# Fixed places behind named loads for the experts' side work, and another division of PSUM

## The chip, the cores and the metric

The kernel runs on one core of one Trainium2 chip. The metric is the device time of one execution in microseconds (us); lower is better. The engines are named as the profile names them: PE is TensorE's matmul, PEld its weight load, DVE is VectorE, ACT is ScalarE, POOL is GpSimd, and SP is SyncE, which here only issues transfers. An engine's issuing sequencer has a q behind its name (SPq).

## The reference, cut to what matters

One layer on 256 tokens of width 2048: a mixing sub-layer (three token mixers behind one projection, gated, summed, projected back), then a mixture of experts. Only the second half is touched by the change:

```python
combine = ...                      # (256 tokens, 16 experts), two weights per token are not zero
y = jnp.zeros_like(t)
for e in range(N_EXPERTS):         # 16 experts
    act = jax.nn.silu(t @ w_gate[e]) * (t @ w_up[e])      # 2048 -> 1024
    y = y + combine[:, e:e + 1] * (act @ w_down[e])       # 1024 -> 2048
x = x + gate_f * y
```

All is float32. An expert's three matrices are 8 MB each, so the 16 experts read 384 MB, which is most of what the kernel reads.

## The kernel before

**Stages.** Up to about 700 us the projections and mixers run; then the output projection, interleaved with the router's inputs; from about 850 us the router's choice; from about 865 us to the end the 16 experts. The kernel is written in a framework that sets the semaphores itself and fixes each engine's instruction order ahead of the run: it walks the program in order of priority with its own model of time, so an instruction whose inputs are ready in that model can be put ahead of one that was traced earlier. `tc.issue_after(ins)` adds an edge of order alone: what is traced in its block on the engine of `ins` comes behind `ins` on that engine.

**Experts.** A token's rows are not run through all experts: each expert has 64 slots (`CAP`). `gather` (matmuls L1071, one-hot `O` against the three bfloat16 parts `h2`) collects the tokens of an expert into `X`, transposed; L1077 and L1079 make their scale `rB`; DVE L1081 and L1083 scale and shift. `scatter` (L1096, ACT L1098) makes `OT`, the same one-hot the other way round.

A *unit* (L1118) multiplies 64 slots by a 128-row-pair slice of weights: one *load* `k2` is 1 MB (L855, issued by SP into the next of the rotating buffers `wr`, `m`, `ws`), and `pair` (L1111) issues its matmuls, 8 instructions in the trace, in two column halves of the array. The gate and the up matrix are a unit of 8 loads each, the down matrix two units (halves) of 4 loads. A unit's sums lie in one PSUM tile of two banks. Behind a unit:

- after gate or up, `hidden` copies the tile to `graw` (ACT L1133) and `rest` turns it round with matmuls (L1138, 16 instructions); then ACT applies Silu (L1146, tile `sgt`) or DVE multiplies (L1152, tile `A`);
- after a half of down, DVE L1164 scales it into `graw`, `split_to` cuts it into two parts `y` (ACT L173, DVE L174), and `combine_part` (two code matmuls L1176 and DVE L1177) adds a 128-token by 512-column part to the result `x2`. An expert has 8 such parts.

The units follow in the order gate(0), then for each expert e: up(e), gate(e+1), down(e) in two halves. The last expert's down matrix is read in another shape, 8 loads in 4 chunks of 512 columns; after each chunk `give_out` combines the chunk before it and sends it out through ACT's queue.

**Side work.** The pieces that stand between units (the gather, `scatter`, `rest`, the parts of combine) are closures in two lists, `soon` and `todo`. After each load's matmuls `between` (L1103) takes one piece off the lists. No edge ties a piece to the load after which it was traced.

**PSUM.** It has 8 banks. Before the experts two pools are closed and one is opened, so that the experts have three unit tiles (`ring`, 6 banks) and two single banks (`mx2`) for all the side work.

**Weight buffers.** 15 buffers of 1 MB rotate in the experts (18 until the first up unit is traced). SP's queue issues a load when the buffer's last reader on PE is done.

Of the kernel before, what the change touches and what calls it, by code (L numbers as in the profile page):

```python
# [53 lines left out]
def kernel(  # L54
# [988 lines left out]
    dve.tensor_copy(xr_i, xr_f)  # L1043

    fnp.close()
    mxbp.close()
    dn.close()


    ringp, ring_pool = open_pool(name="ring", bufs=3, space=PSUM)  # L1050

    def mx2():
        t = mx_pool.tile([P, 512], F32, name="mx")
        return t

    moep, moe = open_pool(name="moep", bufs=2, side="right")
    def ring():
        t = ring_pool.tile([P, 2, 512], F32, name="ring")
        return t

    def gather(O, Or, X, kg=8):

        for g in range(KD // kg):
            ps = mx2()
            for kk in range(kg):
                k2, j = divmod(g * kg + kk, 2)
                o = ps[:, kk * CAP:(kk + 1) * CAP]
                i = 0
                for t in range(NT):
                    for part in h2:  # L1070
                        pe.matmul(o, lhsT=part[:, t, k2 * 256 + j:(k2 + 1) * 256:2], rhs=O[:, t, 0:CAP],  # L1071
                                  start=i == 0, stop=i == 5)
                        i += 1
            if g == 0:
                pr = mx2()
                for t in range(NT):
                    pe.matmul(pr[:, 0:CAP], lhsT=ones, rhs=Or[:, t, :], start=t == 0, stop=t == NT - 1)  # L1077
                rB = moe.tile([P, 1, CAP], F32, name="rB", bufs=1)
                act.copy(rB[:, 0, :], pr[:, 0:CAP])  # L1079
            ks = slice(g * kg, (g + 1) * kg)  # L1080
            dve.tensor_tensor(X[:, ks, :], ps[:, 0:kg * CAP].rearrange("p (k s) -> p k s", s=CAP),  # L1081
                              rB.to_broadcast([P, kg, CAP]), op=ALU.mult)
            dve.tensor_tensor(  # L1083
                X[:, ks, :], X[:, ks, :],
                shT[:, ks].rearrange("p (k o) -> p k o", o=1).to_broadcast([P, kg, CAP]), op=ALU.add)
            yield
# [4 lines left out]

    def scatter(O):

        ps = mx2()
        for t in range(NT):
            pe.matmul(ps[:, t * P:(t + 1) * P], lhsT=O[:, t, :], rhs=ident_b, start=True, stop=True)  # L1096
        OT = moe.tile([P, S], F32R, name="OT", bufs=3)
        act.copy(OT, ps[:, 0:S])  # L1098
        return OT

    soon, todo = [], []

    def between():  # L1103
        for jobs in (soon, todo):
            if jobs:
                return jobs.pop(0)()

    def pair(acc, cc, lhs, k, rhs, last):

        for j in range(2):  # L1110
            pe.matmul(acc[j * CAP:(j + 1) * CAP, cc, :], lhsT=lhs[:, k + j, :], rhs=rhs[j],  # L1111
                      start=k == 0, stop=k == last)

    def drain():
        while soon:
            between()

    def unit(lhs, view, nk2):  # L1118


        acc = ring()
        for k2 in range(nk2):
            raw = load_e(view(k2))
            for cc in range(2):
                pair(acc, cc, lhs, 2 * k2, [raw[:, j * 1024 + cc * 512:j * 1024 + (cc + 1) * 512]
                                            for j in range(2)], 2 * nk2 - 2)
            between()
        return acc

    def hidden(acc):  # L1130

        raw = moe.tile([P, 1024], F32, name="graw", bufs=1)
        act.copy(raw, acc.rearrange("p a b -> p (a b)"))  # L1133

        def rest():
            ps = mx2()
            for b in range(8):
                pe.matmul(ps[:, b * CAP:(b + 1) * CAP], lhsT=raw[:, b * P:(b + 1) * P], rhs=id2[:, 0:CAP],  # L1138
                          start=True, stop=True)
            return ps.rearrange("p (k s) -> p k s", s=CAP)  # L1140
        return rest

    def gate_unit(wg, X):
        rest = hidden(unit(X, lambda k2: wg[:, k2], 8))
        sg = moe.tile([P, 8, CAP], F32, name="sgt", bufs=1)
        soon.insert(0, lambda: act.activation(sg, rest(), AF.Silu))  # L1146
        return sg

    def up_unit(wu, X, sg):
        rest = hidden(unit(X, lambda k2: wu[:, k2], 8))  # L1150
        A = moe.tile([P, 8, CAP], F32, name="A", bufs=1)
        soon.insert(0, lambda: dve.tensor_tensor(A, rest(), sg, op=ALU.mult))  # L1152
        return A

    def flush():
        while soon or todo:
            between()

    def down_unit(wd, A):
        ys = []  # L1160
        for hf in range(2):
            acc = unit(A, lambda k2: wd[:, k2, :, hf * 1024:(hf + 1) * 1024], 4)
            y = moe.tile([P, 1024], F32, name="graw", bufs=1)
            dve.tensor_tensor(y, acc.rearrange("p a b -> p (a b)"), late[0][:, hf * 1024:(hf + 1) * 1024],  # L1164
                              op=ALU.mult)
            yp = late[1].tile([P, 2, 1024], F32R, name="y", bufs=2)
            split_to(yp[:, 0, :], yp[:, 1, :], y)
            ys.append(yp)
        return ys

    def combine_part(OT, cme, parts, n, t):

        cl = slice(n * 512, (n + 1) * 512)
        ps = mx2()
        for i, y in enumerate(parts):
            pe.matmul(ps, lhsT=OT[:, t * P:(t + 1) * P], rhs=y, start=i == 0, stop=i == len(parts) - 1)  # L1176
        dve.scalar_tensor_tensor(x2[:, t, cl], ps, cme[:, t, :], x2[:, t, cl], op0=ALU.mult, op1=ALU.add)  # L1177

    def combine(OT, cme, ys):
        for n in range(4):  # L1180
            parts = [ys[n // 2][:, i, n % 2 * 512:(n % 2 + 1) * 512] for i in range(2)]
            for t in range(NT):
                todo.append(lambda n=n, t=t, parts=parts: combine_part(OT, cme, parts, n, t))

    state = {}

    def prepare(e, kg=8):

        rke = rank[:, :, e:e + 1]
        X = x_tile()  # L1190
        state[e] = [X, None]
        O, Or = (one_hot(rke), slot_scale(rke)) if e else (O0, Or0)
        parts = gather(O, Or, X, kg)

        def weights():
            state[e][1] = scatter(O)
        return [lambda: next(parts, 0)] * (KD // kg) + [weights]

    jobs = prepare(0, 4)
    jobs[0]()  # L1200
# [1 line left out]
    h2_rest(0, late_parts[0])  # L1202
    with tc.issue_after(slot_scale.last.ins), tc.issue_after(sigm.ins):
        h2_rest(1, late_parts[1])
    soon += jobs[2:]
    sg = gate_unit(wg_v[0], state[0][0])
    for e in range(NE - 1):
        soon += prepare(e + 1)
        A = up_unit(wu_v[e], state[e][0], sg)
        if e == 0:  # L1210
            rotate([pl for pl in rot[0] if pl is not wraw2])
            wr2p.close()
            latep, lt = open_pool(name="latep", bufs=1, side="left")
            late.append(lt.tile([P, D], F32, name="gfB"))
            late.append(lt)
            row_bcast(late[0], 3, 0, D)
        sg = gate_unit(wg_v[e + 1], state[e + 1][0])
        assert len(soon) == 1
        combine(state[e][1], cmb[:, :, e:e + 1], down_unit(wd_v[e], A))


    A, OT = up_unit(wu_v[NE - 1], state[NE - 1][0], sg), state[NE - 1][1]
    while todo:
        todo.pop(0)()
    flush()
    OT, cme = OT.bitcast(F32), cmb[:, :, NE - 1:NE]
    y_last = late[1].tile([P, D], F32, name="y", bufs=2)
    wl_v = w_e_down[0, NE - 1].rearrange("(b p) n -> p b n", p=P)

# [5 lines left out]

    for n in range(4):
        cl = slice(n * 512, (n + 1) * 512)
        acc = ring()
        for b0 in (0, 4):
            raw = load_e(wl_v[:, b0:b0 + 4, cl], 4)  # L1240
            for b in (0, 2):
                pair(acc, 0, A, b0 + b, [raw[:, (b + j) * 512:(b + j + 1) * 512] for j in range(2)], 6)
            if n and b0 == 0:
                give_out(n - 1)
        dve.tensor_tensor(y_last[:, cl], acc[:, 0, :], late[0][:, cl], op=ALU.mult)
    give_out(3)

# [1 line left out]
    with tc.If(nc.values_load(xr_i[0:1, NE:NE + 1], min_val=0, max_val=3) > 0):  # L1249
        with tc.For_i(0, NE) as ev:  # L1250
# [5 lines left out]
            with tc.For_i(0, nr):  # L1256
                dve.tensor_scalar(rke, rke, -float(CAP), None, op0=ALU.add)
                O, X = one_hot(rke), x_tile()
                OT = scatter(O)
                list(gather(O, slot_scale(rke), X))  # L1260
                sg = gate_unit(wg_v[bass.ds(ev, 1)][0], X)
                flush()
                A = up_unit(wu_v[bass.ds(ev, 1)][0], X, sg)
                flush()
                combine(OT, cme, down_unit(wd_v[bass.ds(ev, 1)][0], A))
                flush()
        sp.dma_start(out=out_v, in_=x2)


# [25 lines left out]
```

## Time and profile before

| | |
|---|---|
| median of 3 runs | 1851.79 us (1849.91 to 1852.36) |
| the profiled execution: its own time | 1852.96 us |
| its span, first to last instruction | 1851.2 us |
| PE, PEld busy | 1733.7 us (94%), 1050.2 us (57%) |
| DVE, ACT, POOL busy | 914.2 us, 459.0 us, 107.5 us |
| moved | 644.92 MB, mean 348 GB/s |
| TensorE clock granted, mean | 0.989 |

Busy is the time in which an engine has an instruction in work; a matmul's end is modelled by the profiler, so a busy PE need not be at its peak. The mean over the whole span mixes stages with different limits; what the change touches is the stretch from about 860 us on. In a timeline row the bracket is the engine's idle time just before the row, with the instruction whose end released it.

### The profile page before, as it was taken

To read this page: it belongs to the slowest core of one execution; us is meant where nothing else is said; L and a number is where in the kernel's file an instruction comes from. 1 tells how busy PE (TensorE), PEld (TensorE's weight loads), DVE (VectorE), ACT (ScalarE), POOL (GpSimd) and SP (SyncE) were. 2 spreads that over 40 slices of the span, in tenths; PEclk is the share of its full clock that TensorE was granted. 3 is DMA by queue.
4 is the path that set the end of the run, shared out by engine and by line. 5 is a ranking of instruction groups with operands and counts; after the bars stand their busy time and mean duration, and the time that the engine had idled before them with its cause. 6 is when DMAs were issued, how large, how long until landed. Compare 5 with 4: busy or idle time off the path is not lost.

```text
span 1851.2 us, 23367 instructions
## 1 busy us (share of the span) xinstructions
PE 1733.7 (94%) x9747; PEld 1050.2 (57%) x9748; DVE 914.2 (49%) x1114; ACT 459.0 (25%) x598; POOL 107.5 (6%) x101
## 2 busy tenths in 40 slices
PE   5999999999999999998999999999999999999997
PEld 4989789788788888775433343333333433343332
DVE  6769599978888895665032212231223122312222
ACT  2522346663434444452101000100010001000000
POOL 1000030311312102000000000000000000000000
PEclk9999999999999999998999999999999999999999
DMA  9988887669898996957999999999999999999992
GB/s 322 386 319 299 316 272 247 221 226 327 322 338 321 339 351 222 319 181 274 410 415 418 418 415 415 418 418 415 410 410 418 414 400 416 419 400 415 404 405 78
DMA packets 189230, 644.92 MB, mean 348 GB/s; under 512 B 17820, under 2 KB 26432, under 8 KB 155968
## 3 DMA queue, kind: packets, MB, share of 16 engines
q1 hardware_dynamic: 179568, 637.58, 89.2%
q0 software_dynamic: 2128, 3.38, 0.8%
q10 hardware_dynamic: 7424, 2.42, 0.5%
q8 instruction: 78, 1.28, 0.3%
q14 instruction: 32, 0.26, 0.0%
HBM read 641.18 MB, written 2.16 MB: 348 GB/s over the span
## 4 chain that ended last, share of the span: by engine, by line
PE 82%; DVE 9%; issue 3%; ACT 3%; DMA 2%; SPq 1%; POOL 0%; ACTq 0%; DVEq 0%; POOLq 0%
PE ring L1111 35%; PE dn L331 8%; PE dn L332 8%; PE dn L333 8%; PE mx L1176 4%; PE mx L1138 4%; PE dn L370 3%; PE mx L1071 2%; DVE graw L1164 2%; DVE y L174 2%; ACT graw L1133 2%; PE dn L366 1%; DMA wr<-in_w_ada_dram 1%; PE dn L342 1%; PE dn L343 1%
## 5 line engine op out<-in xcount | busy, mean ns | idle before, releaser
L169 DVE TENSOR_TENSOR ws<-wr,ws 128x1024 fp32r<-128x1024 f32 x226 | 290.8, 1291 | 105.8 <-ACT ws L168 104.6
L168 ACT CAST ws<-wr 128x1024 fp32r<-128x1024 f32 x226 | 236.5, 1050 | 302.1 <-PE dn L333 226.2
L1111 PE MATMUL ring<-wr,X 128*64 128x512 f32 x1096 | 253.8, 608 | 0.0
L331 PE MATMUL dn<-ws,hH 128*128 128x512 f32 x480 | 190.2, 396 | 0.9 <-ACT ws L168 0.9
L332 PE MATMUL dn<-ws,hH 128*128 128x512 f32 x480 | 190.3, 396 | 0.8 <-DVE ws L169 0.8
L333 PE MATMUL dn<-ws,hL 128*128 128x512 f32 x480 | 189.9, 396 | 0.0
L1111 PEld LDWEIGHTS ring<-wr,X 128*64 128x64 f32 x1096 | 76.2, 139 | 146.0 <-issue 142.5
L289 DVE SCALAR_TENSOR_TENSOR acc_r<-wr,cs,acc_r 128x1024 f32<-128x1024 f32 x120 | 157.9, 1316 | 1.6 <-DMA wr<-in_w_ada_dram 0.5
L1133 ACT COPY graw<-ring 128x1024 f32<-128x1024 f32 x32 | 32.4, 1012 | 505.2 <-PE ring L1111 505.2
L1111 PE MATMUL ring<-wr,A 128*64 128x512 f32 x576 | 137.2, 603 | 0.0
L1152 DVE TENSOR_TENSOR A<-mx,sgt 128x512 f32<-128x512 f32 x16 | 11.1, 692 | 252.8 <-PE mx L1138 252.8
L1177 DVE SCALAR_TENSOR_TENSOR x<-mx,cmb,x 128x512 f32<-128x512 f32 x128 | 92.0, 746 | 85.1 <-PE mx L1176 85.0
L1111 PE MATMUL ring<-m,X 128*64 128x512 f32 x544 | 129.0, 609 | 0.0
L1017 DVE TENSOR_SCALAR Or<-iota,rank,r2c 128x64 f32<-128x64 f32 x32 | 9.7, 309 | 235.1 <-PE mx L1077 235.0
L1176 PE MATMUL mx<-y,OT 128*128 128x512 f32 x256 | 92.3, 452 | 35.5 <-DVE y L174 21.9
L1138 PEld LDWEIGHTS mx<-id,graw 128*128 128x128 f32 x512 | 61.6, 191 | 81.7 <-ACT graw L1133 59.0
L1176 PEld LDWEIGHTS mx<-y,OT 128*128 128x128 f32 x256 | 41.4, 188 | 108.5 <-ACT y L173 34.6
L331 PEld LDWEIGHTS dn<-ws,hH 128*128 128x128 f32 x480 | 90.3, 188 | 22.0 <-ACT ws L168 1.3
L332 PEld LDWEIGHTS dn<-ws,hH 128*128 128x128 f32 x480 | 90.4, 188 | 21.6 <-DVE ws L169 1.0
L333 PEld LDWEIGHTS dn<-ws,hL 128*128 128x128 f32 x480 | 90.3, 188 | 20.8
L1138 PE MATMUL mx<-id,graw 128*128 128x64 f32 x512 | 69.8, 281 | 31.9 <-ACT graw L1133 31.9
L1164 DVE TENSOR_TENSOR graw<-ring,gfB 128x1024 f32<-128x1024 f32 x30 | 36.7, 1224 | 121.9 <-PE ring L1111 101.8
(406 smaller groups left out, 2436.3 us busy)
## 6 DMA issues: line engine op xcount, KB each, us to landing
wr<-in_w_in_dram SPq DMA_DIRECT2D x89, 1024.0 KB, 7.3
wr<-in_w_e_down_dram SPq DMA_DIRECT2D x72, 1024.0 KB, 12.7
wr<-in_w_e_gate_dram SPq DMA_DIRECT2D x71, 1024.0 KB, 10.9
wr<-in_w_e_up_dram SPq DMA_DIRECT2D x66, 1024.0 KB, 13.2
wr<-in_w_ada_dram SPq DMA_DIRECT2D x64, 1024.0 KB, 6.9
m<-in_w_e_up_dram SPq DMA_DIRECT2D x35, 1024.0 KB, 13.1
m<-in_w_e_gate_dram SPq DMA_DIRECT2D x33, 1024.0 KB, 12.1
wr<-in_w_ada_dram SPq DMA_DIRECT2D x64, 512.0 KB, 8.3
```

Of the source, the lines that this page charges most:

```text
L168: lately[0] = act.copy(h[:, 0:n], raw)
L169: lately[1] = dve.tensor_tensor(l[:, 0:n], raw, h[:, 0:n].bitcast(F32), op=ALU.subtract)
L289: dve.scalar_tensor_tensor(ac, wk, cs[:, k:k + 1], ac, op0=ALU.mult, op1=ALU.add)
L331: pe.matmul(o, lhsT=a, rhs=wH, start=first, stop=False)
L332: pe.matmul(o, lhsT=a, rhs=wL, start=False, stop=False)
L333: lately[2] = pe.matmul(o, lhsT=b, rhs=wH, start=False, stop=last)
L1111: pe.matmul(acc[j * CAP:(j + 1) * CAP, cc, :], lhsT=lhs[:, k + j, :], rhs=rhs[j], start=k == 0, stop=k == last)
L1133: act.copy(raw, acc.rearrange("p a b -> p (a b)"))
L1138: pe.matmul(ps[:, b * CAP:(b + 1) * CAP], lhsT=raw[:, b * P:(b + 1) * P], rhs=id2[:, 0:CAP], start=True, stop=True)
L1164: dve.tensor_tensor(y, acc.rearrange("p a b -> p (a b)"), late[0][:, hf * 1024:(hf + 1) * 1024], op=ALU.mult)
L1176: pe.matmul(ps, lhsT=OT[:, t * P:(t + 1) * P], rhs=y, start=i == 0, stop=i == len(parts) - 1)
L1177: dve.scalar_tensor_tensor(x2[:, t, cl], ps, cme[:, t, :], x2[:, t, cl], op0=ALU.mult, op1=ALU.add)
```

## The change

The lists `soon` and `todo` and `between` go away. A unit is now given a table from load number to pieces, and `beside` traces the pieces of load `k2` behind that load's last matmul, inside `tc.issue_after` of it. The places are:

- load 0 of gate(e+1): the turning round of up(e) and the product `A`; load 0 of the first down half of expert e: that of gate(e+1) and its Silu;
- load 1 of up(e): the whole gather of expert e+1 and its `scatter`;
- load 2 of the second down half of expert e: the four parts of the combine of the first half; load 3 of up(e+1): the four parts of the second half.

The first expert's pieces stand behind loads 0, 1 and 3 of gate(0). PSUM is not divided anew before the experts: unit tiles come from the pool of the projections (`dn`, two tiles of two banks), and the side work uses `mx()`, which takes turns between two pools of two single banks each. In the last expert's chunks both parts of `give_out` stand behind the chunk's first load. The loads, their order, their buffers and all arithmetic stay as they were. The diff, cut to its core:

```diff
-    mxbp.close()
-    dn.close()
-    ringp, ring_pool = open_pool(name="ring", bufs=3, space=PSUM)
-    def mx2():
-        t = mx_pool.tile([P, 512], F32, name="mx")
-        return t
...
-            ps = mx2()
+            ps = mx()
...
     def pair(acc, cc, lhs, k, rhs, last):
         for j in range(2):
-            pe.matmul(acc[...], lhsT=lhs[:, k + j, :], rhs=rhs[j], start=k == 0, stop=k == last)
+            lately[2] = pe.matmul(acc[...], lhsT=lhs[:, k + j, :], rhs=rhs[j], start=k == 0, stop=k == last)
+    def beside(jobs, k2):
+        if k2 in jobs:
+            with tc.issue_after(lately[2].ins):
+                for job in jobs[k2]:
+                    job()
-    def unit(lhs, view, nk2):
-        acc = ring()
+    def unit(lhs, view, nk2, jobs):
+        acc = dn_tile(dn_pool)
         for k2 in range(nk2):
             raw = load_e(view(k2))
             for cc in range(2):
                 pair(...)
-            between()
+            beside(jobs, k2)
         return acc
...
-    sg = gate_unit(wg_v[0], state[0][0])
-    for e in range(NE - 1):
-        soon += prepare(e + 1)
-        A = up_unit(wu_v[e], state[e][0], sg)
+    sg, sg_job = gate_unit(wg_v[0], state[0][0], {0: [jobs[2]], 1: [jobs[3]], 3: [jobs[4]]})
+    held = []
+    for e in range(NE):
+        X, cme = state[e][0], cmb[:, :, e:e + 1]
+        nxt = prepare(e + 1) if e + 1 < NE else []
+        first = {1: nxt, 3: held}
+        if e == 0:
+            first[0] = [sg_job]
+        A, A_job = up_unit(wu_v[e], X, sg, first)
...
-        sg = gate_unit(wg_v[e + 1], state[e + 1][0])
-        assert len(soon) == 1
-        combine(state[e][1], cmb[:, :, e:e + 1], down_unit(wd_v[e], A))
+        if e == NE - 1:
+            break
+        sg, sg_job = gate_unit(wg_v[e + 1], state[e + 1][0], {0: [A_job]})
+        OT = state[e][1]
+        y0 = down_half(wd_v[e], A, 0, {0: [sg_job]})
+        y1 = down_half(wd_v[e], A, 1, {2: [lambda: combine_half(OT, cme, y0, 0)]})
+        held = [lambda OT=OT, cme=cme, y1=y1: combine_half(OT, cme, y1, 1)]
+    A_job()
...
-        acc = ring()
+        acc = dn_tile(dn_pool)
...
             if n and b0 == 0:
-                give_out(n - 1)
+                beside({0: [lambda: give_out(n - 1)]}, 0)
```

## Rows read from the trace of the kernel before

**Rows 1.** Windows: busy us of PE, PEld, DVE, ACT, POOL; clock, DMA share, GB/s.
```profile
1100.00:1300.00 200.00, 185.38 (x1176) 76.17 (x1174) 48.90 (x69) 18.12 (x25) 0.00 (x0) 0.98 1.02 417
...
1500.00:1700.00 200.00, 185.12 (x1102) 74.73 (x1099) 44.60 (x62) 16.90 (x22) 0.00 (x0) 0.99 1.01 410
1700.00:1800.00 100.00, 91.96 (x497) 35.61 (x498) 23.95 (x29) 8.99 (x11) 0.00 (x0) 0.98 1.01 407
```
**Rows 2.** Waits of SP's queue, 900 to 1800 us: total us, times, longest.
```profile
SPq L855 <- PE ring L1111: 719.9, 347, 5.6
```
**Rows 3.** Waits of PE, 900 to 1800 us, all that the view shows.
```profile
PE mx L1138 <- ACT graw L1133: 30.8, 27, 1.2
PE mx L1176 <- DVE y L174: 21.9, 28, 0.9
PE mx L1176 <- ACT y L173: 10.3, 15, 0.7
```
**Rows 4.** DMA issues, 940 to 1000 us: KB each, median us to landing.
```profile
wr<-in_w_e_gate_dram SPq DMA_DIRECT2D x7, 1024.0 KB, 15.7
```
**Rows 5.** DMA issues, 1690 to 1750 us.
```profile
wr<-in_w_e_gate_dram SPq DMA_DIRECT2D x4, 1024.0 KB, 9.7
```
**Rows 6.** Timeline of DVE: `A` of experts 0, 1, 5, 6, 7.
```profile
905.16 0.69 DVE L1152 TENSOR_TENSOR A<-mx,sgt 128x512 f32<-128x512 f32 x1 [10.24 <-PE mx L1138]
958.76 0.69 DVE L1152 TENSOR_TENSOR A<-mx,sgt 128x512 f32<-128x512 f32 x1 [3.04 <-PE mx L1138]
...
1205.33 0.69 DVE L1152 TENSOR_TENSOR A<-mx,sgt 128x512 f32<-128x512 f32 x1 [16.54 <-PE mx L1138]
1267.66 0.69 DVE L1152 TENSOR_TENSOR A<-mx,sgt 128x512 f32<-128x512 f32 x1 [18.23 <-PE mx L1138]
1328.30 0.69 DVE L1152 TENSOR_TENSOR A<-mx,sgt 128x512 f32<-128x512 f32 x1 [16.54 <-PE mx L1138]
```
**Rows 7.** Timeline of PE, 1000 to 1006 us, around one fall of the clock.
```profile
1000.94 0.50 PE L1176 MATMUL mx<-y,OT 128*128 128x512 f32 x1 [0.69 <-ACT y L173]
1002.20 0.50 PE L1176 MATMUL mx<-y,OT 128*128 128x512 f32 x1 [0.76 <-DVE y L174]
1002.63 3.22 PE L1111 MATMUL ring<-m,X 128*64 128x512 f32 x8
```
**Rows 8.** Chain that ended last, 865 to 1000 us: start, us, what.
```profile
905.13 13.88 PE ring L1111 x64
919.01 1.93 PE mx L1138 x16
...
936.80 1.87 PE ring L1111 x8
938.67 1.51 PE mx L1071 x48
...
944.13 0.67 PE mx L1176 x2
```
**Rows 9.** The page, costliest groups: x count | busy us, mean ns | idle before.
```profile
L1177 DVE SCALAR_TENSOR_TENSOR x<-mx,cmb,x 128x512 f32<-128x512 f32 x128 | 92.0, 746 | 85.1 <-PE mx L1176 85.0
```
**Rows 10.** Timeline of SP from 1796 us: the last load's issue ends the row.
```profile
1795.22 5.79 SPq L855 DMA_DIRECT2D wr<-in_w_e_down_dram  x2
```
**Rows 11.** DMA from 1800 us: GB/s in 40 slices; the last load's landing.
```profile
GB/s 386 391 386 386 395 369 238 41 6 0 0 0 0 0 0 0 0 0 0 0 167 35 77 125 0 117 85 20 181 0 58 143 0 202 0 13 236 180 6 0
...
wr<-in_w_e_down_dram SPq DMA_DIRECT2D x1, 1024.0 KB, 10.6
```
**Rows 12.** Chain that ended last, 1810 us to the end.
```profile
1809.63 3.03 PE ring L1111 x14
...
1815.87 0.70 DVE A L1152
...
1829.86 0.70 DVE y L1245
...
1841.36 1.89 PE ring L1111 x8
```

More of the change, by code (lines that the diff above doesn't have):

```diff
@@ L1045 @@
     fnp.close()
-    mxbp.close()
-    dn.close()
-    ringp, ring_pool = open_pool(name="ring", bufs=3, space=PSUM)
-    def mx2():
-        t = mx_pool.tile([P, 512], F32, name="mx")
-        return t
     moep, moe = open_pool(name="moep", bufs=2, side="right")
-    def ring():
-        t = ring_pool.tile([P, 2, 512], F32, name="ring")
-        return t
     def gather(O, Or, X, kg=8):
         for g in range(KD // kg):
-            ps = mx2()
+            ps = mx()
             for kk in range(kg):
@@ L1074, in gather @@
             if g == 0:
-                pr = mx2()
+                pr = mx()
                 for t in range(NT):
@@ L1092, in scatter @@
     def scatter(O):
-        ps = mx2()
+        ps = mx()
         for t in range(NT):
@@ L1099, in scatter @@
         return OT
[L1101 to L1106, printed above, removed]
     def pair(acc, cc, lhs, k, rhs, last):
         for j in range(2):
[L1111 to L1115, printed above, removed]
-            between()
-    def unit(lhs, view, nk2):
-        acc = ring()
+            lately[2] = pe.matmul(acc[j * CAP:(j + 1) * CAP, cc, :], lhsT=lhs[:, k + j, :], rhs=rhs[j],
+                                  start=k == 0, stop=k == last)
+    def beside(jobs, k2):
[5 more added lines that the diff above has]
+        acc = dn_tile(dn_pool)
         for k2 in range(nk2):
@@ L1126, in unit @@
                                             for j in range(2)], 2 * nk2 - 2)
-            between()
+            beside(jobs, k2)
         return acc
@@ L1135, in rest @@
         def rest():
-            ps = mx2()
+            ps = mx()
             for b in range(8):
@@ L1141, in hidden, with gate_unit, up_unit, down_half @@
         return rest
-    def gate_unit(wg, X):
-        rest = hidden(unit(X, lambda k2: wg[:, k2], 8))
+    def gate_unit(wg, X, jobs):
+        rest = hidden(unit(X, lambda k2: wg[:, k2], 8, jobs))
         sg = moe.tile([P, 8, CAP], F32, name="sgt", bufs=1)
[L1146 to L1150, printed above, removed]
+        return sg, lambda: act.activation(sg, rest(), AF.Silu)
+    def up_unit(wu, X, sg, jobs):
+        rest = hidden(unit(X, lambda k2: wu[:, k2], 8, jobs))
         A = moe.tile([P, 8, CAP], F32, name="A", bufs=1)
[L1152 to L1169, printed above, removed]
+        return A, lambda: dve.tensor_tensor(A, rest(), sg, op=ALU.mult)
+    def down_half(wd, A, hf, jobs):
+        acc = unit(A, lambda k2: wd[:, k2, :, hf * 1024:(hf + 1) * 1024], 4, jobs)
+        y = moe.tile([P, 1024], F32, name="graw", bufs=1)
+        dve.tensor_tensor(y, acc.rearrange("p a b -> p (a b)"), late[0][:, hf * 1024:(hf + 1) * 1024],
+                          op=ALU.mult)
+        yp = late[1].tile([P, 2, 1024], F32R, name="y", bufs=2)
+        split_to(yp[:, 0, :], yp[:, 1, :], y)
+        return yp
     def combine_part(OT, cme, parts, n, t):
         cl = slice(n * 512, (n + 1) * 512)
-        ps = mx2()
+        ps = mx()
         for i, y in enumerate(parts):
@@ L1177, in combine_part, with combine_half @@
         dve.scalar_tensor_tensor(x2[:, t, cl], ps, cme[:, t, :], x2[:, t, cl], op0=ALU.mult, op1=ALU.add)
-    def combine(OT, cme, ys):
-        for n in range(4):
-            parts = [ys[n // 2][:, i, n % 2 * 512:(n % 2 + 1) * 512] for i in range(2)]
+    def combine_half(OT, cme, yp, hf):
+        for n in range(2):
             for t in range(NT):
-                todo.append(lambda n=n, t=t, parts=parts: combine_part(OT, cme, parts, n, t))
+                combine_part(OT, cme, [yp[:, i, n * 512:(n + 1) * 512] for i in range(2)], 2 * hf + n, t)
     state = {}
@@ L1189, in prepare, with matrix @@
         rke = rank[:, :, e:e + 1]
-        X = x_tile()
-        state[e] = [X, None]
         O, Or = (one_hot(rke), slot_scale(rke)) if e else (O0, Or0)
-        parts = gather(O, Or, X, kg)
-        def weights():
+        state[e] = [x_tile(), None]
+        parts = gather(O, Or, state[e][0], kg)
+        def matrix():
             state[e][1] = scatter(O)
-        return [lambda: next(parts, 0)] * (KD // kg) + [weights]
+        return [lambda: next(parts, 0)] * (KD // kg) + [matrix]
     jobs = prepare(0, 4)
@@ L1204 @@
         h2_rest(1, late_parts[1])
-    soon += jobs[2:]
-    sg = gate_unit(wg_v[0], state[0][0])
-    for e in range(NE - 1):
-        soon += prepare(e + 1)
-        A = up_unit(wu_v[e], state[e][0], sg)
+    sg, sg_job = gate_unit(wg_v[0], state[0][0], {0: [jobs[2]], 1: [jobs[3]], 3: [jobs[4]]})
[7 more added lines that the diff above has]
+        A, A_job = up_unit(wu_v[e], X, sg, first)
         if e == 0:
@@ L1216 @@
             row_bcast(late[0], 3, 0, D)
-        sg = gate_unit(wg_v[e + 1], state[e + 1][0])
-        assert len(soon) == 1
-        combine(state[e][1], cmb[:, :, e:e + 1], down_unit(wd_v[e], A))
[L1222 to L1226, printed above, removed]
+        if e == NE - 1:
[6 more added lines that the diff above has]
+    A_job()
+    OT = state[NE - 1][1].bitcast(F32)
     y_last = late[1].tile([P, D], F32, name="y", bufs=2)
@@ L1260 @@
                 list(gather(O, slot_scale(rke), X))
[L1261 to L1266, printed above, removed]
+                sg, job = gate_unit(wg_v[bass.ds(ev, 1)][0], X, {})
+                job()
+                A, job = up_unit(wu_v[bass.ds(ev, 1)][0], X, sg, {})
+                job()
+                for hf in range(2):
+                    combine_half(OT, cme, down_half(wd_v[bass.ds(ev, 1)][0], A, hf, {}), hf)
         sp.dma_start(out=out_v, in_=x2)
```

## The prediction

> **What bounds the kernel now.** The page comes first: PE is busy 94% of the span, and the last half of it is the experts' stretch, with PE and DMA both full in every slice. Two full engines cannot both set the pace, so the windows come next: from 1100 us on the DMA share is 1.01 or more, at 417 GB/s at first and 410 and 407 later [rows 1]. A load of 1.0486 MB at 417 GB/s takes 2.51 us, an expert's 24 loads 60.4 us. Then the waits, from both sides. SP's queue waits 720 us of 900 for PE to give a buffer back [rows 2]. PE waits for no load worth a row: all its idle time is for ACT and DVE, 30.8 + 21.9 + 10.3 = 63 us [rows 3]. So PE is the one that sets the pace, and DMA has work queued all the same, because buffers come back just fast enough. How close it is shows in the landings: a load issued between 940 and 1000 us lands 15.7 us later, about six loads of 2.51 us in flight [rows 4]; near 1700 us it is 9.7 us, about four [rows 5]. The buffers that are not in flight hold weights that PE has not got to. PE slowly falls behind.
>
> Last the timeline, for PE's own period. The product `A` is made once an expert. From expert 5 to 6 it takes 62.33 us, from 6 to 7 60.64 us [rows 6]; over all 14 steps from expert 1 (958.76) to 15 (1815.87) the mean is 61.2 us [rows 6, 12]. That is 0.8 us over what DMA needs. The end shows the debt: the last load's issue ends at 1801.0, so it began some 0.4 us before, and it lands 10.6 us later, at 1811.2 [rows 10, 11]; PE starts on its last matmuls at 1841.4, 30 us after [rows 12]. Whatever makes PE quicker in the experts can win until DMA's landings set the end, and no more.
>
> **The change part by part.** *The waits of L1138.* They are 30.8 us, 27 times, 1.1 us each [rows 3]: the turning round is issued ahead of the next unit's first load and stands there until ACT has copied `graw`. Behind load 0 it has that load's matmuls, 1.87 us [rows 8], to hide the 1.1 us. At 900 us / 61.4 us = 14.7 experts in the view this is 2.1 us an expert. If the place did not hold, nothing is gained.
>
> *The waits of L1176.* 32.2 us, 2.2 us an expert [rows 3]: parts of a combine run before ACT and DVE have cut `y`. In the fall of the clock shown they stood one load behind the half's end and missed `y` by 0.69 and 0.76 us [rows 7]. Behind load 2 of the second half it is three loads, behind load 3 of the next up unit four, so 3.5 us more (two loads at 1.74 us) against some 1.5 us missing. Gain 2.2 us. Were a part earlier than its `y`, it would wait up to the 0.8 us of the rows.
>
> *The clock.* The 1.69 us between 62.33 and 60.64 are a stretch at half clock: after waits of 0.69 and 0.76 us close together the 8 matmuls of a load take 3.22 us instead of 1.87 [rows 6 to 8]. Without the waits it should go: 0.85 us an expert.
>
> *Fewer, larger pieces.* A load alone between two pieces takes 1.87 us, in a row of eight 13.88 / 8 = 1.74 us [rows 8], so a place saves about 0.13 us. Some nine places fewer an expert: 1.2 us.
>
> *What an expert costs then.* The trace has one without any wait: from `A` of expert 0 to that of expert 1, 53.6 us [rows 6]. In it only five of the eight parts of a combine ran; three more at 0.67 us [rows 8] give 55.6 us, less the 1.2 us 54.4. The removals give 61.2 - 2.1 - 2.2 - 0.85 - 1.2 = 54.9 us. I take 55 us. DMA needs 60.4: DMA sets the pace, and PE has 5 us an expert to work off its debt. It need not be all: for `A` of expert 15 to come as early as the loads allow (1791 us, below) PE's period must be (1791 - 958.8) / 14 = 59.4 us, so 1.8 us of saving are enough, less than either of the waits with the clock.
>
> *Other PSUM.* The four single banks let the four parts of a combine be issued in a row: a part is 0.67 us of PE [rows 8] and 0.75 us of DVE [rows 9], so with two banks the third and fourth would wait for DVE, at most some 0.8 us a piece of four, 1.6 us an expert, which the 5 us would still cover. Two unit tiles where there were three: a tile is needed again after the next unit, at least 4 loads (7 us) later, and its reader is one pass of ACT or DVE. Nothing; at most, if the reader stood behind the four parts' DVE work, 3 us (4 x 0.75) less what lies between.
>
> *New order, new queues.* The edges are order on PE alone. A piece now stands behind its load, so a late load makes it late, by up to 2.5 us; its readers are far away (`A`, `X` and `sgt` are read 7 or more loads later, `y` has two buffers). The gather in one piece (two times 1.51 us and little more [rows 8]) holds back the next load's matmuls and so the return of one buffer; with several loads in flight DMA does not notice. SP's and POOL's queues issue what they issued. In the last expert nothing hides `rest`; it stays.
>
> *The end.* DMA from 1300 us on ran at 407 to 410, not 417 [rows 1]: 500 us x 7 / 417 = 8.4 us lost at most, if all of it is want of free buffers. The view cannot say which part is; I take half, 4 us, and the last load lands at 1807. The last eight loads go at 386 to 391 GB/s [rows 11], 2.70 us each, so the last up load lands 21.6 us earlier, at 1785.5. Its matmuls (1.9 us) and the chain to `A` (1812.7 to 1815.9, 3.2 us [rows 12]) put `A` at 1791. From there the kernel took 1851.2 - 1815.9 = 35.3 us, PE's chain and not DMA's: from the `y` of chunk 1 (1829.86) to the end of the last chunk's matmuls (1843.25) lie two chunks, 6.7 us each, and a chunk's two loads take 5.4. In three chunks DVE's `y` of 0.70 us [rows 12] now lies beside the chunk's first load: 0.8 us each with its signals, 2.4 us. So the span ends at 1791 + 35.3 - 2.4 = 1823.9 us. The landing itself would allow 1807 + 9.8 (1841.4 to the end) and up to 3.8 us for 1.5 MB of outputs that now share the engines with the loads: 1821, so the chain decides. The profiled execution's time is 1.8 us over its span, and the median 1.2 us under that: 1824.5 us.
>
> **The rivals.** *The clock eats it (slower).* PE, once level with DMA, does 1.74 us and waits 0.77 us at every load. If such waits halve the clock, the 55 us become 55 / (1 - s/2) for a share s of the time at half clock; at s = 0.21 that is the present 61.5 us, and at a third 66 us: 14 x (66 - 61.2) = 67 us more, about 1919 us. For it: two waits of 0.69 and 0.76 us were enough [rows 7]. Against it: waits of 1.1 us alone, at L1138, go by at a mean granted clock of 0.98 [rows 1, 3], and at half clock a load takes 3.22 us, longer than its landing, so PE does not wait and the clock comes back. [...] I give slower 9%.
>
> *The wait moves (smaller gain).* Something of the new order stands on PE: a bank, or `y`. If only 1 us an expert is left, `A` of 15 comes at 1815.9 - 14 = 1802 and the median at 1802 + 35.3 - 2.4 + 0.6 = 1835.5 us. 12%, between 1832 and 1846.
>
> *Nothing changes.* The pieces were already traced behind loads, and the waits of [rows 3] come back at the new places: 1852 us. 5%; against it speaks that the present order has them before their load, which the edge forbids.
>
> **How the numbers follow.** The forecast has 74%: 1824.5 us, 1817 (all 8.4 us of DMA's loss, and no half clock at the last `A`, 2.9 us) to 1831 (no loss recovered, and a few us at half clock at the end). With the smaller gain the range of 8 in 10 is 1816 to 1837 us. A measurement of this kernel tells about 0.2% (3.7 us) from no change. Faster: 74 + 12 = 86%; same 5%; slower 9%.
>
> **What the profile after would show.** L1138 and L1176 gone from PE's waits in the experts, and loads (DMA) in their place; no regular alternation of the steps of `A`; landings of 18 us and more after issue until the end; GB/s at 417 through 1300 to 1780 us; the last load landing near 1807 us and PE on its last matmuls near 1814. Wrong it would be by a granted clock under 0.9 in the experts, by waits of L1176 for DVE, or if the steps of `A` stayed above 60.5 us while SP still waited for PE.

## The result, and the profile after

The changed kernel takes 1826.99 us in the median of 4 runs (1826.09 to 1828.9), the kernel before 1850.85 us beside it (4 runs, 1845.03 to 1852.36): a ratio of 0.9878, 95% interval 0.9855 to 0.9902. The forecast was 1824.5 us in a range of 1816 to 1837. The profiled execution is the slowest of the four, 1828.9 us, with a span of 1827.2 us.

The page of the changed kernel, engines and the chain that ended last:
```profile
PE 1712.1 (94%) x9747; PEld 1050.4 (57%) x9748; DVE 911.6 (50%) x1114; ACT 459.0 (25%) x598; POOL 106.6 (6%) x101
...
PE 48%; DMA 42%; DVE 4%; issue 3%; SPq 1%; POOL 0%; ACT 0%; DVEq 0%; POOLq 0%
```
The same shares of the chain in the kernel before:
```profile
PE 82%; DVE 9%; issue 3%; ACT 3%; DMA 2%; SPq 1%; POOL 0%; ACTq 0%; DVEq 0%; POOLq 0%
```
PE is as full as it was, 94%, and yet in the experts it is no longer what decides: of the chain DMA held 2% and now holds 42%. The share of busy time did not tell the two apart; the chain and the waits do. Those of PE, 900 to 1800 us, the first rows:
```profile
PE dn L1093 <- DMA wr<-in_w_e_down_dram: 17.6, 27, 0.7
PE dn L1093 <- DMA wr<-in_w_e_gate_dram: 13.8, 25, 1.3
PE dn L1093 <- DMA m<-in_w_e_gate_dram: 7.4, 14, 0.9
...
PE mx L1123 <- ACT graw L1118: 1.1, 1, 1.1
```
And those of SP's queue in the same stretch:
```profile
SPq L855 <- PE dn L1093: 126.5, 100, 8.4
SPq L855 <- DMA wr<-in_w_e_up_dram: 123.6, 60, 2.9
SPq L855 <- DMA wr<-in_w_e_down_dram: 68.9, 44, 2.2
```
The 63 us for ACT and DVE [rows 3] are gone but for some 2 us in the last expert, where the turning round was left as it was; PE waits for loads. SP waited 720 us for PE [rows 2], now 126; for most of the rest it waits until an earlier load has landed. The roles are exchanged.

The product `A` shows when this happened (timeline of DVE; experts 0, 1, 2, 3, 4, 5 and 15):
```profile
908.40 0.69 DVE L1137 TENSOR_TENSOR A<-mx,sgt 128x512 f32<-128x512 f32 x1 [12.27 <-PE mx L1123]
961.82 0.69 DVE L1137 TENSOR_TENSOR A<-mx,sgt 128x512 f32<-128x512 f32 x1 [9.33 <-PE mx L1123]
1015.24 0.69 DVE L1137 TENSOR_TENSOR A<-mx,sgt 128x512 f32<-128x512 f32 x1 [9.34 <-PE mx L1123]
1068.66 0.69 DVE L1137 TENSOR_TENSOR A<-mx,sgt 128x512 f32<-128x512 f32 x1 [9.34 <-PE mx L1123]
1128.57 0.69 DVE L1137 TENSOR_TENSOR A<-mx,sgt 128x512 f32<-128x512 f32 x1 [9.33 <-PE mx L1123]
1189.33 0.69 DVE L1137 TENSOR_TENSOR A<-mx,sgt 128x512 f32<-128x512 f32 x1 [9.34 <-PE mx L1123]
...
1795.19 0.69 DVE L1137 TENSOR_TENSOR A<-mx,sgt 128x512 f32<-128x512 f32 x1 [10.32 <-PE mx L1123]
```
Three steps of 53.42 us are PE's own period. In them it gains some 7 us an expert on the loads; in the fourth (59.91) it catches up, and from there the mean step is (1795.19 - 1128.57) / 11 = 60.6 us, the loads'. Before, the steps were 60.64 and 62.33 in turn [rows 6].

Windows (columns as in [rows 1]):
```profile
1100.00:1300.00 200.00, 184.86 (x1190) 76.57 (x1186) 52.66 (x75) 17.52 (x24) 0.00 (x0) 1.00 1.02 417
...
1500.00:1700.00 200.00, 181.81 (x1098) 72.87 (x1096) 43.00 (x60) 17.50 (x23) 0.00 (x0) 1.00 1.02 416
1700.00:1800.00 100.00, 89.57 (x488) 34.75 (x486) 24.77 (x30) 8.40 (x10) 0.00 (x0) 0.98 1.01 408
```
The 417 GB/s that sank to 410 [rows 1] hold to about 1780 us. Behind that come the last expert's loads in their other shape, so that the window up to 1800 has 408 where it had 407. The clock is whole: between 871 and 1796 us the trace has no stretch at half clock (the 0.98 is a fall of 3.4 us at 1796). The DMA issues of 940 to 1000, 1690 to 1750 and from 1798 us (KB each, median us to landing):
```profile
wr<-in_w_e_gate_dram SPq DMA_DIRECT2D x7, 1024.0 KB, 19.8
...
wr<-in_w_e_gate_dram SPq DMA_DIRECT2D x4, 1024.0 KB, 19.8
...
out_dram<-x ACTq DMA_DIRECT2D x8, 256.0 KB, 3.2
wr<-in_w_e_down_dram SPq DMA_DIRECT2D x1, 1024.0 KB, 11.7
```
A load lands 20 us after its issue, early and late, where it had been 15.7 and then 9.7 [rows 4, 5]. From 1200 to 1700 us seven loads are in flight whenever one is issued. Most issues follow the landing of the load eight before within 0.15 us: the loads use eight semaphores in turn, and SP waits for the one that comes next. So eight loads in flight is as far ahead as this program gets. The end of the chain that ended last:
```profile
1790.11 1.96 PE dn L1093 x8
...
1792.09 1.02 ACT graw L1118
...
1793.16 2.01 PE mx L1123 x16
...
1795.19 0.70 DVE A L1137
...
1815.92 1.89 PE dn L1093 x8
```
`A` of the last expert comes 20.7 us earlier than in [rows 12], and the last matmuls 25.4 us. Of the 24.0 us between the two spans, 20.7 are there at the last `A`, 3.3 come behind it.

### The profile page after: what moved, and what is told of

Read it like the earlier page. It is cut to its first block, busy times and chain, and to the rows that moved or that the text cites. A ratio compares the mean times of both kernels' runs of the same rounds, so it can differ in the third digit from the quotient of the medians.

```text
span 1827.2 us, 23422 instructions
## 1 busy us (share of the span) xinstructions
PE 1712.1 (94%) x9747; PEld 1050.4 (57%) x9748; DVE 911.6 (50%) x1114; ACT 459.0 (25%) x598; POOL 106.6 (6%) x101
## 4 chain that ended last, share of the span: by engine, by line
PE 48%; DMA 42%; DVE 4%; issue 3%; SPq 1%; POOL 0%; ACT 0%; DVEq 0%; POOLq 0%
PE dn L1093 10%; PE dn L333 8%; PE dn L332 8%; PE dn L331 8%; DMA wr<-in_w_e_gate_dram 8%; DMA wr<-in_w_e_down_dram 7%; DMA m<-in_w_e_up_dram 6%; DMA wr<-in_w_e_up_dram 6%; DMA ws<-in_w_e_up_dram 3%; DMA ws<-in_w_e_gate_dram 3%; DMA m<-in_w_e_down_dram 3%; PE dn L370 3%; DMA m<-in_w_e_gate_dram 2%; DMA wr<-in_w_ada_dram 2%; DMA ws<-in_w_e_down_dram 2%
## 5 line engine op out<-in xcount | busy, mean ns | idle before, releaser
L1093 PE MATMUL dn<-wr,X 128*64 128x512 f32 x1096 | 253.0, 602 | 15.3 <-DMA wr<-in_w_e_gate_dram 13.8
L1142 DVE TENSOR_TENSOR graw<-dn,gfB 128x1024 f32<-128x1024 f32 x30 | 36.7, 1225 | 369.8 <-PE dn L1093 369.8
L1093 PEld LDWEIGHTS dn<-wr,X 128*64 128x64 f32 x1096 | 73.2, 137 | 171.5 <-issue 118.0
L1093 PE MATMUL dn<-wr,A 128*64 128x512 f32 x576 | 136.6, 601 | 18.6 <-DMA wr<-in_w_e_down_dram 17.6
L1118 ACT COPY graw<-dn 128x1024 f32<-128x1024 f32 x32 | 32.4, 1012 | 468.0 <-PE dn L1093 468.0
L1093 PE MATMUL dn<-m,X 128*64 128x512 f32 x544 | 127.1, 598 | 8.0 <-DMA m<-in_w_e_gate_dram 7.4
L1093 PE MATMUL dn<-ws,X 128*64 128x512 f32 x408 | 94.9, 599 | 7.3 <-DMA ws<-in_w_e_gate_dram 6.3
L1093 PEld LDWEIGHTS dn<-wr,A 128*64 128x64 f32 x576 | 37.7, 136 | 104.5 <-issue 64.5
L340 PE MATMUL dn<-hH,ws 128*128 128x256 f32 x320 | 91.6, 286 | 0.0
L343 PE MATMUL dn<-hH,ws 128*128 128x256 f32 x320 | 90.7, 284 | 0.3 <-DVE ws L169 0.3
L342 PE MATMUL dn<-hL,ws 128*128 128x256 f32 x320 | 90.5, 283 | 0.0
```

The source lines that it names most:

```text
L340: pe.matmul(o, lhsT=a, rhs=xH[:, kx, :], start=first and b % 2 == 0, stop=False, skip_group_check=True)
L342: pe.matmul(o, lhsT=a, rhs=xL[:, kx, :], start=False, stop=False, skip_group_check=True)
L343: pe.matmul(o, lhsT=l, rhs=xH[:, kx, :], start=False, stop=last, skip_group_check=True)
L1093: lately[2] = pe.matmul(acc[j * CAP:(j + 1) * CAP, cc, :], lhsT=lhs[:, k + j, :], rhs=rhs[j], start=k == 0, stop=k == last)
```

## The experiments

Three questions were open. Which part of the change made the gain: the edges, the places, the larger pieces, PSUM? Is the price of a wait its own length, or is all that counts whether PE's period stays under the loads'? And can the 1827 us be lowered? Every ratio is to the kernel before, beside which each set ran (medians 1850.1 to 1853.1 us); "period" is the step of `A` while PE sets the pace.

**No edges** (the changed kernel, places named, order free):
```diff
     if k2 in jobs:
-        with tc.issue_after(lately[2].ins):
-            for job in jobs[k2]:
-                job()
+        for job in jobs[k2]:
+            job()
```


> The kernel after, its pieces traced at the same places, without the edges. The pace theory (what counts is PE's time for an expert, against the 60.4 to 60.8 us that its 24 loads take; the edges are what removes PE's waits): pieces slip ahead of their load again, PE waits some 1.1 us for ACT at each turning round, its period goes from 53.4 towards 58 us or more; if the waits for y come back too it passes 60 us and the time is 1840 to 1851 us. The rival that the place in the program is enough: no waits, 1827 us, 0.988 of before.

Measured: 1824.95 us, 0.9853 (0.9833 to 0.9873), period 59.0 us. Waits of PE, 900 to 1800 us, and the summary of `A` (count, ns min/median/max, first and last start):
```profile
PE mx L1122 <- ACT graw L1117: 31.9, 28, 1.2
PE mx L1152 <- ACT y L173: 5.2, 7, 0.8
PE mx L1152 <- DVE y L174: 4.4, 15, 0.3
```
```profile
L1136 DVE TENSOR_TENSOR A<-mx,sgt x16: 691/691/692, 905.8 to 1793.8; 128x512 f32<-128x512 f32 x16
```
Without the edges the turning round comes ahead of its load again, and its 31 us of waits are all back, as in [rows 3]; of those for `y`, 9.6 us are, where there were 32.2. Nor do the larger pieces hold together. The gather of one expert begins like this (timeline of PE), with a load between its parts:
```profile
1106.92 0.93 PE L1060 MATMUL mx<-O,h 128*128 128x64 bf16 x26
1107.79 1.94 PE L1093 MATMUL dn<-m,A 128*64 128x512 f32 x8
1109.66 0.82 PE L1060 MATMUL mx<-O,h 128*128 128x64 bf16 x22
```
Counted in that timeline, side work stands at 10 places in an expert here, at 5 in the changed kernel and at 11 in the kernel before. The expectation was right on the period (58 us or more) and gave no time for it alone. The whole gain is there all the same, because 59.0 us is still 1.6 under the loads' 60.6. So the edges take 5.6 us off PE's period, but the time does not hang on them.

**Old PSUM in the new order** (three unit tiles, two single banks):
```diff
+    mxbp.close()
+    dn.close()
+    ringp, ring_pool = open_pool(name="ring", bufs=3, space=PSUM)
+    mx_pools[:] = [mx_pool]
...
-        acc = dn_tile(dn_pool)
+        acc = dn_tile(ring_pool)
```


> The kernel after with the old division of PSUM (three unit tiles, two single banks), edges and places kept. Pace theory: the third and fourth part of a combine wait for DVE, at most some 1.6 us an expert more for PE, 55 us against 60.4: still 1827 us, 0.988 of before, PE's waits for DVE at the combine some 10 to 25 us in all. The rival that the division of PSUM brought the gain: waits come back and the time is about 1850 us.

Measured: 1829.29 us, 0.9882 (0.9862 to 0.9902), period 57.5. Each expert costs PE 57.5 - 53.4 = 4.1 us more, where 1.6 at most were expected, and the waits for DVE's `x` (5.6 us in 900, where 10 to 25 were expected) are a small part of it. The timeline of PE shows three of the five pieces cut in two, with two matmuls of the next load between; what such a cut costs, no run measures by itself. The time is the same, because PE's slack covers all of it.

**New PSUM in the old order** (the kernel before, without its division of PSUM):
```diff
-    mxbp.close()
-    dn.close()
-    ringp, ring_pool = open_pool(name="ring", bufs=3, space=PSUM)
...
-        t = mx_pool.tile([P, 512], F32, name="mx")
-        return t
+        return mx()
...
-        t = ring_pool.tile([P, 2, 512], F32, name="ring")
-        return t
+        return dn_tile(dn_pool)
```


> The kernel before with the new division of PSUM alone, lists of pieces as before. Pace theory: its waits are for ACT's copy and for y, not for banks; they stay at about 60 us from 900 to 1800 us, and the time is that of before within 0.2%, 1851 us. The PSUM theory: near 1827 us.

Measured: 1842.8 us, 0.9955 (0.9938 to 0.9971), where no change was expected. Waits of PE, 900 to 1800 us, and one window, here and in the kernel before:
```profile
PE mx L1130 <- ACT graw L1125: 30.1, 27, 1.2
PE mx L1168 <- ACT y L173: 19.3, 28, 0.7
PE mx L1168 <- DVE y L174: 11.4, 28, 0.5
```
```profile
1300.00:1500.00 200.00, 184.57 (x1145) 74.05 (x1141) 49.14 (x67) 16.60 (x22) 0.00 (x0) 1.00 1.02 416
1300.00:1500.00 200.00, 184.78 (x1083) 73.45 (x1084) 49.28 (x67) 16.94 (x22) 0.00 (x0) 0.98 1.01 412
```
The waits are as many as in [rows 3], but the clock is whole, and the steps of `A` from expert 2 to 13 are an even 60.95 us where 62.33 and 60.64 took turns (61.48 in the mean). The edit is worth some 0.45% in the old lists of pieces, and the half clock left the trace with it. It is not the banks alone: with them the framework orders PE otherwise (an expert's gather begins 42 us behind `A` where it had begun 19 us behind it), and of the 10.1 us between the two spans only 5.1 lie in those even steps; the last two steps and the end give 9.1, and 4.1 are lost before expert 2. Why these waits leave the clock alone and those of [rows 7] did not, the trace does not say.

**Waits given back one by one.** In the changed kernel a piece is traced right behind the unit or half that it needs, with an edge that holds the next load's matmuls behind it: the turning round, the combine, or both.
```diff
+        with tc.issue_after(fence[1].ins) if fence[1] else nullcontext():
             for j in range(2):
                 lately[2] = pe.matmul(...)
+        fence[1] = None
...
-        return A, lambda: dve.tensor_tensor(A, rest(), sg, op=ALU.mult)
+        dve.tensor_tensor(A, rest(), sg, op=ALU.mult)
+        fence[1] = fence[0]            # rest's last matmul; Silu likewise
+        return A, lambda: None
...
     def combine_half(OT, cme, yp, hf):
...
+        fence[1] = fence[0]            # the last part's last matmul
...
-        y1 = down_half(wd_v[e], A, 1, {2: [lambda: combine_half(OT, cme, y0, 0)]})
+        y1 = down_half(wd_v[e], A, 1, {0: [lambda: combine_half(OT, cme, y0, 0)]})
-        first = {1: nxt, 3: held}
+        first = {0: held, 1: nxt}
```
The turning round early:

> The kernel after, with the turning round of a gate or up unit put right behind the unit and the next unit's first load behind it by an edge, so that PE stands idle until ACT has copied, about 1.8 us at each of two places an expert. Pace theory: PE's period 53.4 + 3.5 = 57 us, below the loads' 60.4, so nothing but the end is later: 1827 to 1830 us. The rival that each removed wait was paid out in time: 15 experts of 3.5 us, 52 us more, or, if only what it had removed counts, 2.1 us an expert, 31 us more: 1858 us.

Measured: 1827.07 us, 0.9872 (0.9848 to 0.9896), period 55.85 (+2.43). The waits of one such step are 2.3 us.

The combine early:

> The kernel after, with each half's combine behind load 0 of the next unit instead of load 2 or 3, and that unit's next load behind it by an edge, so that PE stands until y is cut: some 1.4 us for its first part and 0.8 for its second, at two places an expert. Pace theory: PE's period 53.4 + 4.4 = 57.8 us, the time that of the kernel after within 0.2%, 1827 us; steps of A of 57 to 58 us at first and 60.6 once level with the loads. The rival that each wait counts: 4.4 us x 15 = 66 us more.

Measured: 1825.41 us, 0.9859 (0.9832 to 0.9886), period 56.12 (+2.70), of which 2.0 us are waits for `y`.

Both:

> Both early places together: the turning round (2.4 us an expert as the run with that alone measured) and the combine (4.4 us). Pace theory: PE's period is 53.4 + 2.4 + 4.4 = 60.2 us and more where the clock falls; over 60.6 it sets the pace again. 1832 to 1850 us, though the two alone cost nothing: the sum is not the sum of the parts. The rival that what counts is the division of PSUM and the size of the pieces: 1827 us as with either alone.

Measured: 1825.59 us, 0.9862 (0.9837 to 0.9888), period 58.53 (+5.11), with three steps of 60.24 among them, where the clock fell (1.71 us each). Waits of PE with both, 900 to 1800 us:
```profile
PE mx L1127 <- ACT graw L1122: 35.3, 31, 1.2
PE mx L1161 <- ACT y L173: 17.4, 23, 1.5
PE mx L1161 <- DVE y L174: 7.4, 27, 0.3
```
60 us of waits for ACT and DVE, against 63 in [rows 3], and still the whole gain, which the last expectation had ruled out by pricing the combine's wait too high (4.4 us an expert for 2.70). What differs apart from the waits is above all the number of pieces, 5 places for 11, and with it 60.64 - 58.53 = 2.1 us an expert. That is a remainder: the order and PSUM differ too, and no run changed the pieces alone. With the falls of the clock rarer, it carries the period under the loads'. With the turning round early the clock also fell seven times, here the window in which it shows most:
```profile
1500.00:1700.00 200.00, 184.31 (x1104) 75.25 (x1102) 42.99 (x60) 17.49 (x23) 0.00 (x0) 0.97 1.02 416
```
The clock is 0.97, and DMA's 416 GB/s are not touched: PE had the slack.

**Less work** (the changed kernel without the combine of experts 0 to 14):
```diff
     def combine_half(OT, cme, yp, hf):
+        return
```


> The kernel after without the combine of experts 0 to 14 (their parts' matmuls and additions are left out, so those experts' share is missing in the output). PE's period would be 53.4 - 4.3 = 49 us. Pace theory: the loads set the pace, so nothing is won but the time in which PE works off its debt: 1823 to 1828 us, 0.987 of before. The rival that PE still sets the pace in the kernel after: 4.3 x 15 = 64 us less.

Measured: 1827.71 us, 0.9873 (0.9851 to 0.9895). The first steps of `A` are 49.0 and 49.3 us, the later ones the loads' 60.3 to 61.3 (the last 59.9). Taking another 4 us of work off PE is worth nothing.

**More work and no wait** (the turning round's matmuls three times over, into the same tile):
```diff
+            for _ in range(3):
-            for b in range(8):
-                pe.matmul(ps[:, b * CAP:(b + 1) * CAP], ...)
+                for b in range(8):
+                    pe.matmul(ps[:, b * CAP:(b + 1) * CAP], ...)
```


> The kernel after with each turning round's matmuls issued three times over (same result). It adds work and no wait: 4 x 1.93 = 7.7 us an expert. Pace theory: PE's period is 53.4 + 7.7 = 61.1 us, over the loads' 60.6, so PE sets the pace from the first expert on: A of expert 15 near 962 + 14 x 61.1 = 1817 us, the end some 32 + 4 us later, 1853 us, the time of before without one of its waits. The rival that waits (and the clock after them), not PE's time as such, were the cost: 1827 to 1831 us.

Measured: 1853.44 us, 1.0013 (1.0003 to 1.0022). SP's waits, 900 to 1800 us, a window, the summary of `A`, and the last expert's turning round in the chain that ended last:
```profile
SPq L855 <- PE dn L1093: 712.9, 349, 7.0
```
```profile
1300.00:1500.00 200.00, 200.00 (x1390) 100.18 (x1388) 53.94 (x75) 18.56 (x25) 0.00 (x0) 1.00 1.02 416
```
```profile
L1138 DVE TENSOR_TENSOR A<-mx,sgt x16: 691/692/692, 912.0 to 1819.4; 128x512 f32<-128x512 f32 x16
```
```profile
1810.71 8.70 PE mx L1124 x48
```
PE waits for nothing, 200.00 us busy of 200 at full clock, every edge and place is there, and the gain is gone. SP waits for PE as in [rows 2]. PE's period, 60.56 us, equals the loads' 60.6, so PE never works off what it is behind at the start. Not all of the loss is the period's: in the last expert nothing hides the turning round, and it takes 8.70 us there for 2.01. Without these 6.7 us some 15.5 of the 22.2 us between the two spans would be left.

**The start: keep the clock up** (22 spare matmuls while PE waits for the router, ahead of the experts):
```diff
+        with tc.issue_after(behind.ins):
+            for _ in range(n):
+                i = pe.matmul(wt[:, 0, :], lhsT=ident_b, rhs=h2[0][:, 0, 0:512], start=True, stop=True)
...
```


> The kernel after, with 22 matmuls of 512 bfloat16 columns into an unused PSUM tile while PE otherwise waits 5.3 us for the router's choice. In the kernel after the clock is at half from 857.6 to 871.3 us, and the first expert's gather and first loads run in it (the first load 3.68 us, not 1.94). Since the loads set the pace, and DMA idles from 865 to 876 us until the first buffers come back, the time should fall by what the buffers come back earlier: about 3 us, 1824 us, granted clock 1.0 through 850 to 875 us. If the clock falls in spite of it, or if the first expert's start hangs on DVE and ACT alone: no change, 1827 us.

Measured: 1825.97 us, 0.9864 (0.9846 to 0.9881). The window of 860 to 880 us, here and in the changed kernel:
```profile
860.00:880.00 20.00, 17.39 (x156) 7.99 (x158) 6.47 (x22) 1.20 (x3) 0.00 (x0) 0.91 0.36 135
860.00:880.00 20.00, 16.94 (x149) 8.70 (x151) 8.63 (x36) 1.21 (x3) 0.00 (x0) 0.72 0.33 121
```
The clock there rose from 0.72 to 0.91; but of the 2.8 us by which `A` of expert 0 is earlier, 2.1 are there before the router's choice already, so that some 0.7 us are left for the clock. PE now stands 2.3 us ahead of the first load's matmuls, where it had stood 1.0. The 3 us expected did not come; against the changed kernel the difference is within the noise.

**The end: the last up matrix ahead of the last but one down matrix**, so that `A` of the last expert is early:
```diff
+        if e == NE - 2:
+            A1, behind = up_unit(wu_v[e + 1], state[e + 1][0], sg, {0: [sg_job]}, x_tile()[:, 0:8, :])
...
```


> The kernel after, with the last expert's up unit ahead of the down unit of the expert before it (loads reordered accordingly; its product lies in a free X buffer), so that the chain from the last up unit through ACT, the turning round and DVE to A is done 8 loads before it is needed. In the kernel after PE starts the last chunks' loads at 1795.9 us, 3 us after their first landed, and the last matmuls 3.2 us after the last landing. If the end is that chain, 3 to 5 us less: 1823 us, the last matmuls within 2 us of the last landing. If the last landing and the output's own chain set the end, 1826 to 1827 us.

Measured: 1827.32 us, 0.9867 (0.9848 to 0.9885), no gain. The end of its chain:
```profile
1801.30 3.77 PE mx L1154 x12
1805.07 3.58 PE dn L1093 x16
...
1816.07 1.89 PE dn L1093 x8
```
`A` is made at 1737 us, but a combine of the expert before now stands in the tail (the 12 matmuls at 1801.30), and the last matmuls start as late as in the changed kernel (1815.92).

**Start and end together:**

> Both of the former together. If the two ends of the loads' stretch are independent, the sum: 6 to 8 us under the kernel after, 1820 us, 0.9835 of before. If only one of them holds, 1823 to 1824 us.

Measured: 1824.16 us, 0.9852 (0.9836 to 0.9868). The interval overlaps with that of the changed kernel; the 1820 us expected were not reached, and no run here is faster than the changed kernel beyond the noise.

## Why the prediction was right

**The view of the bound held.** PE sets the pace, DMA comes close behind, and PE may gain only until the landings decide. The runs show it as one curve. By the period of `A` while PE sets the pace, 49.0, 53.4, 55.9, 56.1, 57.5, 58.5 and 59.0 us all give 1825 to 1829 us. The changed kernel's `A` takes (1795.19 - 908.40) / 15 = 59.1 us a step as the loads allow it. Counted from expert 1, as the prediction did, it is 59.5; the prediction had 59.4 as the point from which the saving is enough. Above that point the time rises with the period. At 60.56 us `A` of the last expert comes 24.2 us later than in the changed kernel (3.6 of them at expert 0 already, up to 6.7 for the turning round in the last). At 60.95 us with a first expert of 53.58 it comes 13.4 us later, and the span is 1841.1 - 1827.2 = 13.9 us longer.

**The waits and the pieces.** The period was to fall to 55 us and fell to 53.42. The waits of L1138 were priced at 2.1 us an expert (given back they cost 2.43), those of L1176 at 2.2 (2.70), the clock at 0.85 (1.71 a fall, in every second expert), the pieces at 1.2 (a remainder of 2.1). The last was the one mis-sized: six places fewer, not nine, and each worth some 0.35 us and not the 0.13 taken from the chain, if the remainder is all theirs. The prediction's own wait-free expert says the same: with all eight parts it would take 55.6 us, and the changed kernel's takes 53.42. The misses did not move the time: from a mean of 61.48 us (62.33 and 60.64 in turn) to 59.1 there are 2.4 us, and by these figures any two of the four are enough. The run with both waits given back shows it for the pieces and most of the clock, the run without edges for most of the waits for `y` and the clock. The clock alone is not enough, as the new PSUM in the old order shows (1842.8 us); whether one of the others alone would be, no run shows.

**PSUM.** In the new order it moved nothing, as forecast, though with the old division an expert cost PE 4.1 us more and not the 1.6 us at most; the slack covers that too. In the old lists it moved 0.45%, which the forecast did not have: the order changed with the division, and the clock no longer fell.

**"Nothing changes" was argued wrongly.** It was held against that rival that the old order has the pieces before their load, "which the edge forbids". Without the edge they do go before their load, the waits of L1138 return, the pieces come apart, and the time stays: the edge was not needed. The rival fell for another reason: with the pieces traced at the new places, fewer of the waits for `y` come back and the clock holds, and 59.0 us is low enough.

**The clock rival fell.** PE waits for loads at many places, two of them here (timeline of PE in the changed kernel):
```profile
1316.42 1.94 PE L1093 MATMUL dn<-wr,X 128*64 128x512 f32 x8 [0.29 <-DMA wr<-in_w_e_gate_dram]
1319.62 1.94 PE L1093 MATMUL dn<-wr,X 128*64 128x512 f32 x8 [1.26 <-DMA wr<-in_w_e_gate_dram]
```
Yet the granted clock is 1.00 in these windows, with 60 us of such waits in 900 us, 102 of them and none above 1.3 us. The Trainium skill (TensorE: Matmul & The Clock Gate, section "HAM oscillation — how this bites in real kernels") tells of a kernel in which each burst is shorter than the wait for DMA behind it, and which falls back to half clock at every burst. Here the waits are shorter than the bursts of 1.94 us, so no run here shows that case. Where the clock did fall, with the turning round early, it cost nothing.

**The end.** The last load was to land at 1807 us and landed at 1812.6. What was off is the start it was worked from: the loads restarted at 876.4 us where they had at 872.6, 3.8 us later. Of these, 2.6 were there before the experts, where nothing was changed, so that is the scatter between executions; 1.2 arose in the first expert, whose half clock lasted 13.7 us and not 10.2. The recovery in the middle was 3.9 us. That 4 had been forecast is luck, for it was half of the 8.4 that could be recovered at most, taken because the view could not tell; a part of the 8.4 belongs to the last loads' shape and stayed, as the 408 GB/s up to 1800 us show (and 1300 to 1500 us had run at 412, not at 410 or less). At the very end 1.1 us were lost: the last load landed 3.84 us after the one before it, with outputs in flight beside it, where in the kernel before the first output was issued 14.6 us after the last landing.

From the last `A` the kernel took 32.0 us (forecast 32.9), by sizes that were off both ways. The places of the output pieces are worth 3.6 us and not 2.4. From `A` to the last matmuls it is 22.7 us without the edges (`A` at 1793.78) and 19.0 with them, in the run with the turning round early (`A` at 1795.90), neither with a fall of the clock on the way; the two last matmuls:
```profile
1816.45 1.89 PE dn L1093 x8
1814.93 1.89 PE dn L1096 x8
```
The changed kernel's 20.7 us hold a fall of 3.4 us in which some 1.7 are lost, and behind the last matmuls it took 11.3 us, not the 9.8 of before. So the profiled span came 3.3 us over the forecast one, and the median, which is 1.9 us under that execution, 2.5 us over the forecast.

## What to carry to other kernels

When two engines look full, measure each one's period over a repeated piece of work, and how far it is behind at the start: only what shortens the period of the one that sets the pace can win, and only until the other one's period is reached. A removed wait is not a gain by its length: several small savings may be more than is needed, and a run that adds work without any wait tells period from wait at once. Before an order is enforced, ask how much of the period the time needs: here the edges took 5.6 us off it, and the time was the same without them.

## What the runs showed of the hardware

The clock fell or held by details that no count of waits shows. With 63 us of waits before it fell in every second expert [rows 6]; with 64 us, another division of PSUM and another order it never did between 900 and 1800 us; with 35 us of waits for ACT and some for loads (the turning round early) it fell seven times.

A load of 1 MB landed every 2.49 us in the gate and up matrices, every 2.56 in the down matrices and every 2.70 in the last one, read in 512-column chunks (medians of the changed kernel's landings, with seven others in flight). The three differ in the shape of the read, which no run varied by itself.

With eight loads in flight, SP waited some 2 us at an issue for an earlier one to land (123.6 us in 60 times for one group of loads), so a stream that DMA limits looks like waiting there too; only the name of what is waited for tells the two apart.
